# Low parts of streamed weights: a VectorE subtraction replaced by a negated copy on ScalarE and an accumulating DMA

## The chip, the cores and the metric

The kernel runs on one core of a Trainium2 chip. The metric is device time in microseconds of one execution. Three runs of the kernel before gave 1240.68, 1240.82 and 1240.99 us; the median is 1240.82 us.

A core has five engines with a queue each, which run their instructions in order and wait for one another by semaphores: TensorE (PE; its weight loads are shown as PEld), VectorE (DVE), ScalarE (ACT), GpSimd (POOL) and SyncE (SP), which here only issues DMAs. A DMA can be issued on SP, ACT or POOL; sixteen DMA engines move the data.

## The reference

The reference is a two-layer encoder trunk on one sequence of 512 tokens with 1024 features, in float32.

```python
for l in range(DEPTH):                       # DEPTH = 2
    h = rms_norm(x, norm1_g[l])
    proj = h @ w_in[l]                       # 1024 x 3584
    rq, rk, rv, rg, sq, sk, sv = jnp.split(proj, IN_SPLITS, axis=-1)
    ret = chunk_retention(apply_rotary(rq), apply_rotary(rk), rv)      # 4 heads of 128
    ret = head_group_norm(ret, ret_norm_g[l]) * jax.nn.silu(rg)
    sb = head_rms_norm(stick_breaking(sq, sk, sv), sb_norm_g[l])       # 4 heads of 128
    x = x + jnp.concatenate([ret, sb], axis=-1) @ w_out[l]             # 1024 x 1024
    h = rms_norm(x, norm2_g[l])
    x = x + (jax.nn.silu(h @ w_gate[l]) * (h @ w_up[l])) @ w_down[l]   # d_ff = 2816
return rms_norm(x, final_g)
```

## The kernel before

x is held transposed: eight tiles x[k] of 128 features by 512 tokens. Matrix products keep float32 precision by splitting each operand a into a high part (a rounded to the type fp32r, 12 bits of mantissa) and a low part (a minus the high part). A product is three matmuls: high by high, high by low, low by high (`mm3`). So TensorE needs the high part of a weight first and its low part with the second or third matmul of the first block.

All weights come in one stream, the tensor ws of 204 units; a unit is 128 partitions by 1024 columns of float32 (512 KB), in the order of use (`block_plan`, `unit_plan`). It holds eight blocks of 128x128, or two blocks of 128x512 where a weight is the moving operand (the value projections `proj_v`, and w_down in layer 1). `WeightStream.load` issues a unit's load on SP into one of three buffers wraw; `WeightStream.split` has ScalarE copy it to whi (line 124) and VectorE subtract whi from wraw into wlo (line 125); whi and wlo have three buffers each. `WeightStream.block` hands out the blocks. When the first block of unit u is asked for, it calls the split of the units up to u + 2 and the load of the one after. A buffer of whi or wlo is free when TensorE has used the last block of the unit three before.

The order of TensorE's work is fixed by the program (`Stream`): a main stream of projections, with the attention of each head put in as side tasks after a set delay. The order on the other engines is chosen by a scheduler when the kernel is built.

In most of the kernel TensorE uses the units one after the other. At the end of a `proj_v` and of each column half of w_down in layer 1, the last four blocks are used token block by token block, so that the results of a token block are complete early; the units of these four blocks (two of them, or three where the blocks don't begin at a unit's edge) are all held until the last token block:

```python
for f in fs[: FH - tail]:                 # tail = 4, FH = 11
    w = wst.block("w_down", l, f, dh * 512, 512)
    for tb in range(TB): step(tb, f, w)
rest = [(f, wst.block("w_down", l, f, dh * 512, 512)) for f in fs[FH - tail :]]
for tb in range(TB):
    for f, w in rest: step(tb, f, w)
```

The attention's own operands are split too. Those of q, k and the squares for the head norms have their low parts made on GpSimd (qlo, klo, slo), those of the score weights and the mixed heads on VectorE (ptlo, mlo). `mixed` (retention) computes m on VectorE (line 561), `normed` the square and its parts shi and slo (lines 460, 273, 274), which TensorE sums over the head with a matrix of ones (`finish`).

Of the kernel before, what the change touches and what calls it, by code (L numbers as in the profile page):

```python
# [10 lines left out]
F32 = mybir.dt.float32  # L11
F32R = mybir.dt.float32r
BF16 = mybir.dt.bfloat16
AF = mybir.ActivationFunctionType
ALU = mybir.AluOpType
# [18 lines left out]
BIG = float(2.0**100)  # L34
RQ, RK, RV, RG, SQ, SK, SV = (512 * i for i in range(7))

# the triangle of score blocks, by bank: block rows of [query, key], and of [key, query]
BY_QUERY = ((3,), (2, 0), (1,))
BY_KEY = ((0,), (1, 3), (2,))
WARM = 10  # L40
# [2 lines left out]


def block_plan():
    """Weight blocks in the order of their use: (tensor, layer, k tile, column, width)."""
    plan = []

    def cols(name, l, col):
        return [(name, l, k, col, P) for k in range(KT)]  # L50

    for l in range(L):
        plan += [("w_in", l, k, SV, 512) for k in range(KT)]
        for h in range(NH):
            for c in (SQ, SK, RG):
                plan += cols("w_in", l, c + h * HD)
        plan += [("w_in", l, k, RV, 512) for k in range(KT)]
        for h in range(NH):
            plan += cols("w_in", l, RQ + h * HD) + cols("w_in", l, RK + h * HD)
        for d in range(KT):  # L60
            plan += [("w_out", l, NH + k, d * P, P) for k in range(NH)]
        for d0 in range(0, KT, 4):
            ds = range(d0, d0 + 4)
            plan += [("w_out", l, k, d * P, P) for d in ds for k in range(NH - 1)]
            plan += [("w_out", l, NH - 1, d * P, P) for d in ds]
        for k in range(KT):
            for f in range(2):
                plan += [("w_gate", l, k, f * P, P), ("w_up", l, k, f * P, P)]
        for half in range(2):
            fs = range(half * FH, half * FH + FH)  # L70
            for f in fs:
                if f >= 2:
                    plan += cols("w_gate", l, f * P) + cols("w_up", l, f * P)
            if l < L - 1:
                for d in range(KT):
                    plan += [("w_down", l, f, d * P, P) for f in fs]
            else:
                for dh in range(2):
                    plan += [("w_down", l, f, dh * 512, 512) for f in fs]
    return plan  # L80
# [11 lines left out]


class WeightStream:
    """Loads the weights ahead of their use and splits each into two 12-bit parts."""

    AHEAD = 3

# [16 lines left out]
    def split(self, upto, step=UW):  # L115
        nc = self.nc
        self.load(upto)
        for i in range(len(self.ready), min(upto, len(self.units))):
            raw, w = self.raw[i]
            hi = self.pool.tile([P, UW], F32R, tag="whi", name=f"whi{i}", bufs=3)  # L120
            lo = self.pool.tile([P, UW], F32R, tag="wlo", name=f"wlo{i}", bufs=3)
            for a in range(0, w, step):
                c = slice(a, min(a + step, w))
                nc.scalar.copy(out=hi[:, c], in_=raw[:, c])  # L124
                nc.vector.tensor_tensor(  # L125
                    out=lo[:, c], in0=raw[:, c], in1=hi[:, c].bitcast(F32), op=ALU.subtract
                )
            self.ready.append((hi, lo))

    def block(self, *key):  # L130
# [9 lines left out]


class Stream:
    """The order of the tensor engine's work: side tasks are put into the main stream
    when enough of it has passed for their operands to be ready."""

    def __init__(self, nc):
        self.nc = nc
# [51 lines left out]
def layers(ctx, tc, xT_in, ws_in, gcol_in, gfin_in, cos_in, sin_in, dec_in, out):  # L199
    nc = tc.nc  # L200
# [8 lines left out]
    NG = 24  # L209

    def table(inst):
        """Keeps the scalar engine's table functions in the order of the program."""
        tc.stamp_issue_order_token(inst.ins, "table")
        return inst

# [15 lines left out]
    x = [keep.tile([P, S], F32, name=f"x{k}", tag=f"x{k}") for k in range(KT)]  # L231
    nc.sync.dma_start(out=x[0], in_=xT_in[:, 0, :])
    wst.load(1, step=512)
    for k in range(1, KT):
# [12 lines left out]
    eps = const.tile([P, 1], F32, name="eps")  # L247
# [4 lines left out]
        out=mask16, in_=mask16, compare_op=ALU.is_gt, fill=-BIG,  # L252
# [6 lines left out]
    rs = keep.tile([P, S], F32, name="rs")  # L259
# [20 lines left out]
            )  # L280

    def feed(k, g):
        """x tile k is complete: its gained and split copy, and its squares."""
        split(hhi[k], hlo[k], x[k], gcol[:, g + k : g + k + 1])
        if k == 0:
            nc.scalar.activation(out=ssq, in_=x[k], func=AF.Square)
        else:
            q = small.tile([P, S], F32, tag="sqx", name="sqx", bufs=2)
            nc.scalar.activation(out=q, in_=x[k], func=AF.Square)  # L289
            nc.gpsimd.tensor_tensor(out=ssq, in0=ssq, in1=q, op=ALU.add)  # L290

    def rsqrt(out, ss, n, act=nc.scalar.activation):
        """out = (ss / n + eps) ** -0.5, from exp and ln and a Newton step."""
        shape = list(ss.shape)
        tag = "" if shape[1] == S else str(shape[1])
        r = small.tile(shape, F32, tag="r" + tag, name="r" + tag, bufs=1)
        u = small.tile(shape, F32, tag="u" + tag, name="u" + tag, bufs=1)
        act(out=r, in_=ss, func=AF.Ln, scale=1.0 / n, bias=eps)
        act(out=r, in_=r, func=AF.Exp, scale=-0.5)
        nc.vector.scalar_tensor_tensor(  # L300
            out=u, in0=r, scalar=-0.5 / n, in1=r, op0=ALU.mult, op1=ALU.mult
        )
        nc.vector.scalar_tensor_tensor(
            out=u, in0=ss, scalar=n * EPS, in1=u, op0=ALU.add, op1=ALU.mult
        )
        nc.vector.scalar_tensor_tensor(
            out=out, in0=u, scalar=1.5, in1=r, op0=ALU.add, op1=ALU.mult
        )

    def token_scale():  # L310
        """rs[:, t] = rsqrt(mean of x[t]^2 + eps), the same on every partition."""
        hi, lo = (small.tile([P, S], F32R, tag="sqx", name=n, bufs=2) for n in ("sshi", "sslo"))
        split(hi, lo, ssq)
        ps = bank("o", 1)
        pe.mm(ps, ones_r, hi, True, False)
        pe.mm(ps, ones_r, lo, False, True)
        rsqrt(rs, ps, DM, act)
# [11 lines left out]
    def attention(l):  # L329
        g0 = l * NG  # L330
        with tc.tile_pool(name=f"at{l}", bufs=1, reuse_waits="tile") as sb:
# [23 lines left out]
                return ps  # L355

            def proj_v(col, evac):
                """[token, column] products, the last k tiles by token block."""
                pss = banks_a() if col == SV else [bank() for _ in range(3)] + [bank("z", 4)]
                v = [  # L360
                    sb.tile([P, TB, S], F32R, tag=n, name=n, bufs=1) for n in ("vhi", "vlo")
                ]

                def step(tb, k, w):
                    c = slice(tb * P, tb * P + P)
                    pe.mm3(pss[tb], (hhi[k][:, c], hlo[k][:, c]), w, k == 0, k == KT - 1)

                for k in range(KT - 4):
                    w = wst.block("w_in", l, k, col, 512)
                    for tb in range(TB):  # L370
                        step(tb, k, w)
                ws = [(k, wst.block("w_in", l, k, col, 512)) for k in range(KT - 4, KT)]
                done = []
                for tb in range(TB):
                    for k, w in ws:
                        step(tb, k, w)
                    done.append(tb)
                    if col == SV and tb == 0:
                        continue
                    if col == SV and tb == 1:  # L380
                        scales()
                    while done:
                        i = done.pop(0)
                        evac(i, pss[i], v[0][:, i], v[1][:, i])
                return v
# [33 lines left out]
                return parts(r, tag)  # L419

            def outer(ps, a, b, ca, cb, last=True):
                """ps = a[:, ca].T @ b[:, cb] for split a and b."""
                n = cb.stop - cb.start
                if n == P:
                    pe.mm(ps, a[0][:, ca], b[0][:, cb], True, last)
                else:
                    pe.mm(ps, a[1][:, ca], b[1][:, cb], True, False)
                    pe.mm(ps, a[1][:, ca], b[2][:, cb], False, False)
                    pe.mm(ps, a[2][:, ca], b[1][:, cb], False, last)
# [8 lines left out]
                return hi, lo  # L438

            def weighted(wt, v, h):  # L440
                """o[e, t] = sum over s of v[s, e] wt[s, t], by blocks of s."""
                o = bank("o", 1)
                e = slice(h * HD, h * HD + HD)
                for js, (hi, lo) in zip(BY_KEY, wt):
                    a = 0
                    for j in js:
                        c = slice(a, a + S - j * P)
                        a = c.stop
# [6 lines left out]
            mix = {}  # L455

            def normed(o, m, key):
                """m, o by head with its gains, times the rsqrt of o's mean squares."""
                sq = temp("sq")
                nc.scalar.activation(out=sq, in_=o, func=AF.Square)  # L460
                shi = sb.tile([P, S], F32R, tag="shi", name="shi", bufs=1)
# [335 lines left out]
```

## Time and profile before

| | |
|---|---|
| median of three runs | 1240.82 us |
| span of the profiled execution, first to last instruction | 1238.8 us |
| what the median has above that span | 2.0 us |
| TensorE busy | 1220.4 us, 99% |
| VectorE busy | 693.5 us, 56% |
| ScalarE busy | 488.8 us, 39% |
| GpSimd busy | 165.7 us, 13% |
| data moved by DMA | 115.74 MB, 93 GB/s |

Busy time says how much of the span an engine had an instruction in work. Matmuls overlap and their ends are modelled, so 99% does not mean that TensorE runs at its peak; it means that it hardly ever stands still. PEclk is the clock that TensorE was granted, as a share of full speed. The profiled execution is one of its own, with its span alone; the three timed runs are timed from outside and hold some 2 us around that span.

### The profile page before, as it was taken

How to read it: one execution, taken by the hardware profiler on the slowest of the kernel's cores; microseconds unless marked ns; L12 is line 12 of the kernel's file. 1: busy time of each engine (PE TensorE's matmuls, PEld its weight loads, DVE VectorE, ACT ScalarE, POOL GpSimd, SP SyncE). 2: the span in 40 equal slices, each digit the busy share in tenths (PEclk: the TensorE clock that was granted, in tenths of full speed). 3: DMA queues.
4: the chain of work that ended last, by engine and by line, in shares of the span. 5: the costliest groups of instructions: out<-in, count | busy, mean ns of one | idle time of the engine just before them, and what ended most of it. 6: DMA issues, size and time to landing. Idle time of an engine off the chain costs nothing.

```text
span 1238.8 us, 13898 instructions
## 1 busy us (share of the span) xinstructions
PE 1220.4 (99%) x5474; PEld 999.2 (81%) x5474; DVE 693.5 (56%) x861; ACT 488.8 (39%) x708; POOL 165.7 (13%) x142
## 2 busy tenths in 40 slices
PE   8999999999999999999999999999999999999997
PEld 5888887888888888888888888878888888888886
DVE  5557799775443244444444778997644433444433
ACT  5557553453322123223334766345432312223323
POOL 3221154130000000000112212422100000000011
PEclk9999999999999999999999999999999999999999
DMA  6221231232322323322232222223322322332221
GB/s 238 86 80 57 85 102 58 80 101 87 102 100 87 102 86 101 102 93 96 91 129 86 69 69 85 85 69 102 103 85 89 99 83 94 113 102 87 101 85 69
DMA packets 33329, 115.74 MB, mean 93 GB/s; under 512 B 3824, under 2 KB 3824, under 8 KB 33264
## 3 DMA queue, kind: packets, MB, share of 16 engines
q1 hardware_dynamic: 33120, 114.83, 28.1%
q8 instruction: 43, 0.70, 0.2%
q14 instruction: 22, 0.18, 0.0%
q10 hardware_dynamic: 144, 0.02, 0.0%
HBM read 112.75 MB, written 2.10 MB: 93 GB/s over the span
## 4 chain that ended last, share of the span: by engine, by line
PE 94%; DVE 4%; issue 1%; DMA 1%; ACT 1%; POOL 0%; SPq 0%; DVEq 0%; ACTq 0%
PE acc L178 72%; PE z L178 16%; PE o L178 5%; PE z L189 1%; DMA wraw<-ws 1%; DVE ptlo L274 1%; DVE wlo L125 1%; DVE hlo L277 0%; DVE u L300 0%; DVE mlo L274 0%; POOL slo L274 0%; DVE m L561 0%; DVE t L416 0%; DVE t L414 0%; DVE p L552 0%
## 5 line engine op out<-in xcount | busy, mean ns | idle before, releaser
L124 ACT CAST whi<-wraw 128x1024 fp32r<-128x1024 f32 (+1 forms) x205 | 214.6, 1047 | 505.7 <-PE acc L178 237.2
L178 PE MATMUL acc<-hhi,whi 128*128 128x512 f32 x960 | 376.0, 392 | 0.0
L178 PE MATMUL acc<-hhi,wlo 128*128 128x512 f32 x960 | 373.9, 389 | 0.0
L178 PE MATMUL acc<-hlo,whi 128*128 128x512 f32 x960 | 373.6, 389 | 0.0
L125 DVE TENSOR_TENSOR wlo<-wraw,whi 128x1024 fp32r<-128x1024 f32 (+1 forms) x205 | 258.1, 1259 | 135.8 <-ACT whi L124 134.7
L178 PEld LDWEIGHTS acc<-hhi,wlo 128*128 128x128 f32 x960 | 180.2, 188 | 37.8
L178 PEld LDWEIGHTS acc<-hhi,whi 128*128 128x128 f32 x960 | 180.3, 188 | 36.2
L178 PEld LDWEIGHTS acc<-hlo,whi 128*128 128x128 f32 x960 | 180.3, 188 | 36.0
L665 DVE TENSOR_TENSOR u<-acc,rs 128x512 f32<-128x512 f32 x40 | 27.7, 692 | 134.5 <-PE acc L178 134.5
L290 POOL TENSOR_TENSOR ssq<-ssq,sqx 128x512 f32<-128x512 f32 x28 | 44.8, 1600 | 397.0 <-ACT sqx L289 396.3
L662 DVE TENSOR_TENSOR g<-acc,rs 128x512 f32<-128x512 f32 x40 | 27.7, 692 | 89.9 <-PE acc L178 89.9
L178 PE MATMUL acc<-ahi,wlo 128*128 128x512 f32 x176 | 69.8, 396 | 0.0
L178 PE MATMUL acc<-alo,whi 128*128 128x512 f32 x176 | 69.8, 396 | 0.0
L178 PE MATMUL acc<-ahi,whi 128*128 128x512 f32 x176 | 69.8, 396 | 0.0
L730 POOL TENSOR_TENSOR xtd<-xtd,gfin 128x512 f32<-128x512 f32 x7 | 10.1, 1447 | 349.3 <-ACT fsq L726 349.3
L277 DVE SCALAR_TENSOR_TENSOR hlo<-x,gcol,hhi 128x512 fp32r<-128x512 f32 x32 | 38.6, 1224 | 9.0 <-ACT hhi L276 9.0
L178 PEld LDWEIGHTS acc<-alo,whi 128*128 128x128 f32 x176 | 33.1, 188 | 8.1
L178 PEld LDWEIGHTS acc<-ahi,whi 128*128 128x128 f32 x176 | 33.1, 188 | 8.1
L178 PEld LDWEIGHTS acc<-ahi,wlo 128*128 128x128 f32 x176 | 33.1, 188 | 8.1
L273 ACT CAST ahi<-u 128x512 fp32r<-128x512 f32 x44 | 27.3, 621 | 28.1 <-DVE u L666 28.1
L178 PE MATMUL acc<-mhi,wlo 128*128 128x512 f32 x88 | 36.2, 411 | 0.0
L178 PE MATMUL acc<-mlo,whi 128*128 128x512 f32 x88 | 36.0, 409 | 0.0
(189 smaller groups left out, 1819.0 us busy)
## 6 DMA issues: line engine op xcount, KB each, us to landing
wraw<-ws SPq DMA_DIRECT2D x203, 512.0 KB, 3.5
x<-xT SPq DMA_DIRECT2D x8, 256.0 KB, 7.4
dec<-dec SPq DMA_DIRECT2D x8, 256.0 KB, 4.1
out<-ob SPq DMA_DIRECT2D x4, 512.0 KB, 2.6
wraw<-ws SPq DMA_DIRECT2D x2, 256.0 KB, 3.8
cosrs<-cos SPq DMA_DIRECT2D x2, 256.0 KB, 5.3
sinrs<-sin SPq DMA_DIRECT2D x2, 256.0 KB, 5.4
gfin<-gfin SPq DMA_DIRECT2D x1, 512.0 KB, 4.5
```

Of the source, the lines that this page charges most:

```text
L124: nc.scalar.copy(out=hi[:, c], in_=raw[:, c])
L125: nc.vector.tensor_tensor(out=lo[:, c], in0=raw[:, c], in1=hi[:, c].bitcast(F32), op=ALU.subtract)
L178: self.nc.tensor.matmul(ps, lhsT=lhsT, rhs=rhs, start=start, stop=stop)
L189: self.nc.tensor.transpose(out, src, ident)
L273: nc.scalar.copy(out=hi, in_=src)
L274: eng.tensor_tensor(out=lo, in0=src, in1=hi.bitcast(F32), op=ALU.subtract)
L277: eng.scalar_tensor_tensor(out=lo, in0=src, scalar=scale, in1=hi.bitcast(F32), op0=ALU.mult, op1=ALU.subtract,)
L290: nc.gpsimd.tensor_tensor(out=ssq, in0=ssq, in1=q, op=ALU.add)
L662: nc.vector.tensor_tensor(out=g, in0=pg, in1=rs, op=ALU.mult)
L665: nc.vector.tensor_tensor(out=u, in0=pu, in1=rs, op=ALU.mult)
L730: nc.gpsimd.tensor_tensor(out=y, in0=y, in1=gfin[:, c], op=ALU.mult)
```

## The change

From unit 4 on the low part is made in another way. ScalarE writes the negated high part into wlo (a copy of wraw with the factor -1, which is rounded as the high part is). Then a DMA issued on GpSimd reads the unit from memory a second time and adds it to what stands in wlo. Units 0 to 3 keep the subtraction on VectorE. The loads into wraw stay; a wraw buffer is now free when ScalarE has read it twice.

```diff
                 nc.scalar.copy(out=hi[:, c], in_=raw[:, c])
-                nc.vector.tensor_tensor(
-                    out=lo[:, c], in0=raw[:, c], in1=hi[:, c].bitcast(F32), op=ALU.subtract
-                )
+                if i < 4:
+                    nc.vector.tensor_tensor(
+                        out=lo[:, c], in0=raw[:, c], in1=hi[:, c].bitcast(F32), op=ALU.subtract
+                    )
+                else:
+                    nc.scalar.activation(out=lo[:, c], in_=raw[:, c], func=AF.Copy, scale=-1.0)
+                    nc.gpsimd.dma_start(out=lo[:, c], in_=self.ws[i, :, c], accum_op=ALU.add)
             self.ready.append((hi, lo))
```

The rest of the diff only removes comments. Lines after 127 stand four lines further down in the changed kernel, so that line 273 is 277 there.

The scheduler places the new instructions among the others. ScalarE before, at the change of column halves in the last w_down (whi is a unit's high part, fsq the squares for the last norm, xtd the output by token block):

```order
L124 CAST whi_8844<-wraw_8818 128x1024 [waits DMAHW5_49,DVE_49,PE_49]
L726 ACTIVATE fsq,fss_6752<-xtd_6748 128x512 [waits DVE_49]
L726 ACTIVATE fsq,fss_6753<-xtd_6749 128x512 [waits DVE_49]
L124 CAST whi_8862<-wraw_8848 128x1024 [waits DMAHW6_49,PE_49,Activation_49]
L726 ACTIVATE fsq,fss_6754<-xtd_6750 128x512 [waits DVE_49,Activation_49]
L124 CAST whi_8868<-wraw_8866 128x1024 [waits DMAHW7_49,PE_49]
```

And now at the same place, where wlo on line 130 is the negated copy:

```order
L124 CAST whi_9038<-wraw_9012 128x1024 [waits PE_49,Activation_49]
L730 ACTIVATE fsq,fss_6888<-xtd_6884 128x512 [waits DVE_49]
L730 ACTIVATE fsq,fss_6889<-xtd_6885 128x512 [waits DVE_49]
L130 ACTIVATE wlo_9058<-wraw_9043 128x1024 [waits DMAHW6_49,DMASW0_49,PE_49]
L124 CAST whi_9057<-wraw_9043 128x1024 [waits PE_49,Activation_49]
L730 ACTIVATE fsq,fss_6890<-xtd_6886 128x512 [waits DVE_49,Activation_49]
L130 ACTIVATE wlo_9065<-wraw_9062 128x1024 [waits DMAHW7_49,DMASW1_49,PE_49]
```

Each unit has two instructions on ScalarE, and here the negated copy stands ahead of the high part; the order among the rest is the same.

GpSimd before, in the late attention of layer 0 (q and k are rotated queries and keys, qlo and klo their low parts, slo that of the squares of a head):

```order
L418 TENSOR_TENSOR k<-t_1701,t_1702 128x512 [waits DVE_49]
L274 TENSOR_TENSOR klo<-k,khi 128x512 [waits PE_49,Activation_49]
L418 TENSOR_TENSOR q<-t_1759,t_1760 128x512 [waits DVE_49,PE_49]
L274 TENSOR_TENSOR slo<-sq,shi 128x512 [waits Activation_49]
L274 TENSOR_TENSOR qlo<-q,qhi 128x512 [waits Activation_49]
```

And now at the same place:

```order
L131 DMA wlo_1738<-ws 128x1024 [waits DMASW5_49,Activation_49]
L422 TENSOR_TENSOR k<-t_1725,t_1726 128x512 [waits DVE_49]
L278 TENSOR_TENSOR klo<-k,khi 128x512 [waits Activation_49]
L131 DMA wlo_1797<-ws 128x1024 [waits DMASW6_49,Activation_49]
L422 TENSOR_TENSOR q<-t_1784,t_1785 128x512 [waits DVE_49,PE_49]
L278 TENSOR_TENSOR slo<-sq,shi 128x512 [waits Activation_49]
L278 TENSOR_TENSOR qlo<-q,qhi 128x512 [waits Activation_49]
```

The DMA issues stand among GpSimd's additions and subtractions, each with a wait for ScalarE's negated copy, and what comes after one in the queue starts after it.

## Rows read from the trace of the kernel before

**Rows 1.** The page's busy times of the engines, with share and number of instructions.

```profile
PE 1220.4 (99%) x5474; PEld 999.2 (81%) x5474; DVE 693.5 (56%) x861; ACT 488.8 (39%) x708; POOL 165.7 (13%) x142
```

**Rows 2.** Stretches of 4 us: length, busy times, granted clock, DMA share, GB/s.

```profile
192.00:196.00 4.00, 3.58 (x20) 2.97 (x19) 3.83 (x6) 1.55 (x2) 1.28 (x1) 1.00 0.24 97
200.00:204.00 4.00, 1.66 (x7) 0.85 (x6) 3.87 (x7) 3.68 (x7) 1.93 (x2) 1.00 0.16 67
204.00:208.00 4.00, 4.00 (x12) 3.13 (x11) 3.95 (x5) 1.50 (x3) 1.24 (x1) 0.57 0.02 8
...
808.00:812.00 4.00, 1.66 (x6) 0.88 (x5) 3.87 (x7) 4.00 (x8) 2.30 (x2) 0.98 0.05 20
812.00:816.00 4.00, 4.00 (x12) 3.08 (x12) 3.57 (x4) 1.13 (x2) 0.86 (x1) 0.59 0.17 30
```

**Rows 3.** Timeline, 188 to 204: start, length, engine, line, tiles, [idle before <-releaser].

```profile
188.96 1.23 DVE L125 TENSOR_TENSOR wlo<-wraw,whi 128x1024 fp32r<-128x1024 f32 x1
...
196.65 1.23 DVE L125 TENSOR_TENSOR wlo<-wraw,whi 128x1024 fp32r<-128x1024 f32 x1
...
199.49 0.74 DVE L561 SCALAR_TENSOR_TENSOR m<-o,gcol,gate 128x512 f32<-128x512 f32 x1
...
202.07 1.47 POOL L274 TENSOR_TENSOR slo<-sq,shi 128x512 fp32r<-128x512 f32 x1 [3.06 <-ACT shi L273]
...
203.60 0.50 PE L178 MATMUL o<-slo,ones_r 128*128 128x512 f32 x1 [1.05 <-POOL slo L274]
```

**Rows 4.** Groups by shape: xcount, busy us, mean ns, idle us before and releasers.

```profile
L125 DVE TENSOR_TENSOR wlo<-wraw,whi 128x1024 fp32r<-128x1024 f32 x203 | 256.8, 1265 | 135.5 <-ACT whi L124 134.5
...
L124 ACT CAST whi<-wraw 128x1024 fp32r<-128x1024 f32 x203 | 213.5, 1052 | 505.7 <-PE acc L178 237.2 <-issue 176.6 <-PE z L178 58.4
```

**Rows 5.** DMA: queue with packets, MB, share; issues; the tile wraw's landing times.

```profile
q1 hardware_dynamic: 33120, 114.83, 28.1%
...
wraw<-ws SPq DMA_DIRECT2D x203, 512.0 KB, 3.5
...
DMA to landing us min/median/max: 3.3/3.5/8.3
```

**Rows 6.** SP's waits (us in total, times, longest), and its issues: ns min/median/max.

```profile
SPq L112 <- DVE wlo L125: 1088.4, 197, 12.3
...
L112 SPq DMA_DIRECT2D wraw<-ws x205: 327/328/749, 1.2 to 1203.1; - x103
```

**Rows 7.** Timeline of ScalarE in the feed-forward part of layer 0.

```profile
322.62 1.05 ACT L124 CAST whi<-wraw 128x1024 fp32r<-128x1024 f32 x1 [3.86 <-issue]
...
328.06 1.05 ACT L124 CAST whi<-wraw 128x1024 fp32r<-128x1024 f32 x1 [3.11 <-PE acc L178]
```

**Rows 8.** Timeline at the change of column halves, w_down of layer 1.

```profile
1017.18 1.05 ACT L124 CAST whi<-wraw 128x1024 fp32r<-128x1024 f32 x1 [10.85 <-DVE xtd L723]
...
1022.12 0.40 PE L178 MATMUL z<-wlo,ahi 128*128 128x512 f32 x1
```

**Rows 9.** Timeline after two proj_v of layer 0, and after w_down's first half.

```profile
35.19 1.05 ACT L124 CAST whi<-wraw 128x1024 fp32r<-128x1024 f32 x1
...
41.90 0.39 PE L178 MATMUL acc<-hhi,wlo 128*128 128x512 f32 x1
...
145.48 1.05 ACT L124 CAST whi<-wraw 128x1024 fp32r<-128x1024 f32 x1
...
152.51 0.39 PE L178 MATMUL acc<-hhi,wlo 128*128 128x512 f32 x1
...
1048.68 1.05 ACT L124 CAST whi<-wraw 128x1024 fp32r<-128x1024 f32 x1 [8.75 <-PE z L178]
...
1055.78 0.39 PE L178 MATMUL acc<-hhi,wlo 128*128 128x512 f32 x1
```

**Rows 10.** Timeline of the fourth stick-breaking head of layer 0: GpSimd, then TensorE.

```profile
112.97 1.65 POOL L274 TENSOR_TENSOR klo<-k,khi 128x512 fp32r<-128x512 f32 x1 [5.59 <-ACT khi L273]
...
116.05 0.40 PE L178 MATMUL z<-klo,qhi 128*128 128x512 f32 x1
```

## The prediction, made before the changed kernel ran

> **What bounds the kernel now.** I read the page's busy table first: TensorE is busy 99% of the span, VectorE 56%, ScalarE 39%, GpSimd 13% [rows 1]. So the time is TensorE's matmul stream plus the few places where it stops or runs at its lower clock, and an edit to another engine counts only where TensorE waits for it. The table of stretches shows the largest such place: at the end of each attention part TensorE is idle for some 2.3 us, and in the 4 us after that its granted clock is 0.57 to 0.59, a fall towards the lower of its two levels [rows 2]. The timeline says who is late there: VectorE, whose queue holds a weight subtraction (wlo, line 125) at 188.96 and another at 196.65, then the product m at 199.49; from m come the square and its split slo on GpSimd, and TensorE starts only when slo ends [rows 3]. Everywhere else the weights are early: in the feed-forward part ScalarE copies a unit's high part every 5.44 us, for use two units later [rows 7].
>
> **What goes.** From unit 4 on, 200 of the 204 units lose a subtraction of 1.265 us [rows 4], 253 us of VectorE. Nearly all of it lies beside TensorE's work and is worth nothing. In the late stretch two of them, 2 x 1.23 us, stand before m [rows 3]. Without them m, slo and TensorE come up to 2.46 us earlier, against 0.42 + 2.34 = 2.76 us of idle time in layer 0, and 2.34 in the last stretch of layer 1 [rows 2]. If the stop shrinks to a few tenths the clock should not fall either: 4 us x (1 - 0.57) = 1.7 us more. That bounds the gain at about 4.2 us a layer, 8.3 in all; the lower bound is nothing, if slo comes late for another reason. I take 3.5 a layer, 7 in all, because a few tenths of the wait are not covered. The subtraction that TensorE waits for at the start belongs to unit 3, which keeps it.
>
> **What is added.** ScalarE gets 200 negated copies of 128x1024. Its cast of that shape takes 1.052 us [rows 4], so 210 us more, and ScalarE goes from 39% to 56% busy. GpSimd gets 200 DMA issues. The DMA engines get 200 x 512 KB from memory again, plus a read of the same 512 KB in the destination, since an addition into the destination needs both. The important part is latency. Before, a low part was ready about 1.2 us after its high part. Now it is ready when the negated copy is written, GpSimd has issued, and the DMA has landed. I call the last two together T.
>
> T has no row. A plain load of the same size lands in 3.5 us, between 3.3 and 8.3 [rows 5]. Its packets take 0.281 x 1238.8 x 16 / 33120 = 0.168 us; at 9 packets for each engine that is 1.5 us of moving data [rows 5]. The second read adds 1.5. SP's load of a later unit waits for line 125 today, 197 times [rows 6], so it will wait for the negated copy and start at the same moment as the accumulation; sharing the 16 engines adds another 1.5. An issue takes 0.33 us on SP [rows 6]; I put 0.3 for GpSimd's. T = 3.5 + 1.5 + 1.5 + 0.3 = 6.8 us. The bounds are the plain load's own 3.3 and its worst 8.3; above that an addition that moves slowly through the DMA engines cannot be excluded by any row. I take 6.8, as the sum of the parts. Data volume alone doesn't bind: 28.1% x 3 = 84% of the engines' time.
>
> The Trainium skill (DMA: Bandwidth & Descriptors, Anatomy of one DMA — SWDGE (gpsimd) path) fits a DMA issued on GpSimd as 2.0 us plus its bytes over 436 GB/s, an estimate of 3.2 us for 512 KB. No run here shows such a DMA; the plain loads on SP, at 3.5, agree with it within a tenth. With 3.2 for T nothing below would be late; that is the first rival's world.
>
> **Where T is covered and where not.** In the steady stream a unit's buffer comes free two units before its successor is wanted: 2 x 5.44 us less high and negated copy (2.1) leaves 8.8 us for T [rows 7]. So 6.8 is hidden in most of the kernel. It is not where a block of matmuls holds two or three of the three buffers to its end, which happens in seven places, each time with the negated copy placed first on ScalarE:
> - w_down of layer 1, between the two column halves (two places). ScalarE starts the next unit at 1017.18 and TensorE wants its low part at 1022.12 [rows 8]; less 1.05 for the copy and 0.1 for a semaphore, 3.8 us are left. Short by 3.0 us each, 6.0. A stop of that size brings the clock down as in [rows 2], 1.7 each, 3.4.
> - After proj_v of the stick-breaking heads, both layers: 35.19 to 41.90 [rows 9], 5.55 left, short by 1.25, 2.5 in both.
> - After proj_v of the retention heads, both layers: 145.48 to 152.51 [rows 9], 5.9 left, short by 0.9, 1.8 in both.
> - From w_down's first half to the gate columns in layer 1: 1048.68 to 1055.78 [rows 9], 5.95 left, short by 0.85.
> Together 6.0 + 3.4 + 2.5 + 1.8 + 0.85 = 14.6 us.
>
> The DMA issue also stands in GpSimd's queue and waits there for ScalarE's negated copy; behind it are the splits qlo, klo and slo, for which TensorE waits. In the tightest of four heads klo ends at 114.62 and is wanted at 116.05 [rows 10]: 1.4 us of cover, against 1.05 for a negated copy ahead of khi and 0.3 for the issue. That I cost at nothing; if an issue holds GpSimd for 1 us, it costs 0.6 us in each layer. In the late attention stretch the negated copy stands on ScalarE before mhi, in time that is idle there, so it does not delay slo.
>
> The sum, made on the profiled span: 1238.8 - 7 + 14.6 = 1246.4. The median of the runs is 2.0 above that span, so about 1248.5 by the median; 1248 is predicted, some 0.6% slower.
>
> **Rivals.**
> First, the accumulation lands like a plain load: T of 3.3 to 4.3. For it: the fixed part of 3.5 us is by far the larger one, and rows show no cost of an addition. Against it: two streams have to be read and the raw load starts beside it. Then the seven places cost under 1 us and the relief of VectorE stays: 1240.8 - 7 = 1234, or 1232.5 with the full 8.3.
>
> Second, T of about 5, no contention with the raw load. Two places are short by 1.2, with one clock fall each at most: 2.4 + 3.4 - 7 = -1.2, so 1239.6, no difference to be told (0.2%, 2.5 us, is about what a measurement of this kernel tells from no change).
>
> Third, on the slow side, the accumulating DMA is slow enough to bound the stream: T above 8.8. Each buffer then turns once in 16.3 + (T - 8.8) us, so every unit costs (T - 8.8) / 3 more, over some 180 units. At T = 9: 12 us, and the seven places 38, less 7: 1284. At T = 10: 72 + 46 - 7, so 1352. The DMA engines themselves bind when an added DMA takes more than (100 - 28.1) / 28.1 = 2.6 times the packet time of a plain one; I assumed twice, which is near. Against it: each of the 16 engines has only some 32 KB to add for each unit.
>
> **How the numbers follow.** Forecast, T between 6 and 8: 0.40, from 1243 (T = 6: 9 - 7) to 1265 (T = 8: 31 - 7). First rival 0.24, second 0.15, third 0.21. Faster by over 0.2%: the first rival and a little of the second, 0.27. Within 0.2%: the rest of the second and the foot of the forecast, 0.14. Slower: the forecast and the third rival, 0.59. The range has to reach the first rival at 1232 and into the third, up to T just over 9: 1300. The forecast's own range is 1243 to 1265.
>
> **What would show it.** In the profile after: the DMA table has a second 512 KB row issued on GpSimd, whose time to landing plus issue is T; 6 to 8 is right, under 5 or over 9 wrong. TensorE waits with an accumulating DMA as the releaser, longest in the two column-half changes of w_down in layer 1, near 1018 and 1200, by some 3 us, and a clock row near 0.6 behind each. The idle time near 200 and 810 us is down to a few tenths, with the clock staying at 1.0. ScalarE near 56%, VectorE near 36%. Waits of TensorE for klo or slo would show that GpSimd's queue, not T, is what costs. Waits for the low part in every feed-forward unit would be the third rival; none at all in the seven places the first.

## The result and the profile after

The changed kernel takes 1276.2 us (median of four runs, 1274.1 to 1278.1), against 1240.75 us for the kernel before on the same chip: 1.0289 times as long, 95% interval 1.0273 to 1.0306, or 35.5 us slower. Predicted were 1248 us. The direction is the predicted one; the loss is nearly five times the predicted 7.2 us, and the time lies above the forecast's own range, 1243 to 1265. The four runs of the changed kernel form two pairs, near 1274.2 and 1278.1 us, and the profiled execution, with a span of 1276.3 us, belongs to the longer pair.

The busy times, which answer to [rows 1], came out near what was expected for ScalarE and VectorE (53% and 35% for 56% and 36%):

```profile
PE 1231.4 (96%) x5474; PEld 1002.8 (79%) x5474; DVE 442.7 (35%) x661; ACT 670.2 (53%) x908; POOL 321.8 (25%) x342
```

The DMA table, which answers to [rows 5] (queue with packets, MB and share; issues with count, size and median us to landing), and the view of the tile wlo with its landing times, in us from the start of GpSimd's issue:

```profile
q0 software_dynamic: 28800, 104.87, 46.7%
...
wraw<-ws SPq DMA_DIRECT2D x203, 512.0 KB, 6.3
wlo<-ws POOLq DMA_DIRECT2D x200, 512.0 KB, 7.7
```

```profile
DMA to landing us min/median/max: 5.2/7.7/10.2
```

A packet of the accumulation holds a DMA engine for 0.467 x 1276.3 x 16 / 28800 = 0.331 us, twice the 0.168 us of a plain one, as the prediction assumed. The landing takes 7.7 us at the median. The plain load that runs beside it went from 3.5 to 6.3 us. The issue itself is a row on GpSimd (columns as in [rows 4]):

```profile
L131 POOL DMA_DIRECT2D wlo<-ws x200 | 173.8, 869 | 780.2 <-ACT wlo L130 766.0
```

What TensorE waited for (us in total, times, longest), first the view of the whole span and then of the last 276 us alone:

```profile
PE acc L182 <- DMA wlo<-ws: 13.0, 8, 4.2
PE z L182 <- DMA wlo<-ws: 10.1, 5, 3.3
PE o L182 <- POOL slo L278: 3.6, 4, 1.5
...
PE z L182 <- ACT khi L277: 2.8, 2, 1.4
PE z L182 <- POOL klo L278: 1.4, 2, 0.7
```

```profile
PE acc L182 <- DMA wlo<-ws: 8.5, 4, 4.2
PE z L182 <- DMA wlo<-ws: 7.7, 3, 3.3
```

So 16.2 of the 23.1 us of waiting for accumulations lie after 1000 us, nearly all of it in w_down of layer 1. The timeline there (start, length, engine, line, tiles, [idle before <-releaser]) names the places:

```profile
1025.05 0.50 PE L182 MATMUL acc<-wlo,ahi 128*128 128x512 f32 x1 [1.59 <-DMA wlo<-ws]
...
1028.76 0.50 PE L182 MATMUL acc<-wlo,ahi 128*128 128x512 f32 x1 [2.06 <-DMA wlo<-ws]
...
1043.74 0.50 PE L182 MATMUL z<-wlo,ahi 128*128 128x512 f32 x1 [2.81 <-DMA wlo<-ws]
...
1065.38 0.50 PE L182 MATMUL z<-wlo,ahi 128*128 128x512 f32 x1 [1.64 <-DMA wlo<-ws]
...
1222.18 0.50 PE L182 MATMUL acc<-wlo,ahi 128*128 128x512 f32 x1 [4.20 <-DMA wlo<-ws]
...
1239.15 0.50 PE L182 MATMUL z<-wlo,ahi 128*128 128x512 f32 x1 [3.27 <-DMA wlo<-ws]
```

Those at 1043.74 and 1239.15 are the changes of column halves that the prediction named ([rows 8]). The other four are inside a column half, where the four held blocks begin. None of them was predicted.

Stretches (columns as in [rows 2]): the late attention, the feed-forward part, and the 4 us behind the first change of column halves.

```profile
200.00:204.00 4.00, 4.00 (x22) 3.48 (x21) 3.87 (x8) 2.82 (x6) 2.19 (x3) 1.00 0.70 173
204.00:208.00 4.00, 4.00 (x19) 3.25 (x18) 2.92 (x2) 2.85 (x4) 2.91 (x3) 1.00 0.45 86
320.00:360.00 40.00, 40.00 (x179) 33.10 (x178) 9.00 (x13) 17.67 (x21) 6.05 (x7) 1.00 0.88 196
...
1044.00:1048.00 4.00, 4.00 (x13) 3.15 (x13) 0.00 (x0) 0.00 (x0) 0.00 (x0) 0.65 1.04 271
```

The stop near 200 us is gone and the clock stays up there. In the feed-forward part TensorE is busy for 40.00 of 40 us: the steady stream is covered. Behind the long stop at 1043.74 the clock is granted at 0.65.

The order of TensorE's matmuls is the same in both kernels, so the start times of the same matmul in the two traces can be set side by side. The difference grows or shrinks in steps. The steps, in us, with the clock's part inside:

| place | predicted | measured |
|---|---|---|
| the seven places of the prediction: column-half changes 9.7, ends of proj_v SV 4.0 and RV 1.7, gate 0.9 | +14.6 | +16.3 |
| starts of the held blocks in w_down of layer 1 | 0 | +11.8 |
| start of layer 1, in proj_v of the stick-breaking heads, near 630 to 645 | 0 | +4.9 |
| slo of stick-breaking heads | 0 | +4.7 |
| stop in the late attention goes, both layers | -7 | -9.8 |
| khi and klo of the next head, 10 us later, both layers | 0 | +8.5 |
| sum | +7.6 | +36.4 |

The spans differ by 1276.3 - 1238.8 = 37.5; 1.1 us is in steps too small to place. With those steps counted to the place where they lie, single rows move by up to half a microsecond (12.3 for 11.8, -10.3 for -9.8). The steps are those of one execution, too: of the last row, some 3 us are falls of the clock behind khi, and experiments 7 and 8, with the same waits of 1.4 us there, show none; the stop of 4.20 us at 1222.18 is 2.8 and 2.0 us at the same matmul in these two, whose w_down is unchanged.

### The profile page after: what moved, and what is told of

Read it like the earlier page. It is cut to its first block, busy times and chain, and to the rows that moved or that the text cites. A ratio compares the mean times of both kernels' runs of the same rounds, so it can differ in the third digit from the quotient of the medians.

```text
span 1276.3 us, 14285 instructions
## 1 busy us (share of the span) xinstructions
PE 1231.4 (96%) x5474; PEld 1002.8 (79%) x5474; DVE 442.7 (35%) x661; ACT 670.2 (53%) x908; POOL 321.8 (25%) x342
## 3 DMA queue, kind: packets, MB, share of 16 engines
q0 software_dynamic: 28800, 104.87, 46.7%
## 4 chain that ended last, share of the span: by engine, by line
PE 60%; issue 24%; DMA 5%; POOL 5%; ACT 3%; DVE 3%; SPq 0%; POOLq 0%; ACTq 0%; DVEq 0%
PE acc L182 47%; PE z L182 9%; DMA wlo<-ws 5%; POOL wlo L131 4%; PE o L182 3%; ACT wlo L130 1%; PE z L193 1%; DMA wraw<-ws 1%; ACT whi L124 0%; DVE hlo L281 0%; DVE m L475 0%; DVE e L508 0%; POOL slo L278 0%; DVE u L304 0%; DVE x L610 0%
## 5 line engine op out<-in xcount | busy, mean ns | idle before, releaser
L131 POOL DMA_DIRECT2D wlo<-ws x200 | 173.8, 869 | 780.2 <-ACT wlo L130 766.0
L130 ACT ACTIVATE wlo<-wraw 128x1024 fp32r<-128x1024 f32 x200 | 210.9, 1055 | 79.0 <-PE z L182 43.9
L294 POOL TENSOR_TENSOR ssq<-ssq,sqx 128x512 f32<-128x512 f32 x28 | 40.3, 1440 | 33.1 <-ACT sqx L293 31.8
L709 DVE TENSOR_TENSOR x<-x,acc 128x512 f32<-128x512 f32 x16 | 11.0, 687 | 95.2 <-PE acc L182 95.2
L182 PE MATMUL z<-wlo,ahi 128*128 128x512 f32 x88 | 36.5, 415 | 7.7 <-DMA wlo<-ws 7.7
L278 DVE TENSOR_TENSOR alo<-u,ahi 128x512 fp32r<-128x512 f32 x44 | 30.4, 692 | 35.5 <-ACT ahi L277 35.3
L182 PE MATMUL z<-wlo,hhi 128*128 128x512 f32 x80 | 33.4, 418 | 5.8 <-DVE wlo L126 3.3
```

Of the source, the lines that this page charges most:

```text
L130: nc.scalar.activation(out=lo[:, c], in_=raw[:, c], func=AF.Copy, scale=-1.0)
L131: nc.gpsimd.dma_start(out=lo[:, c], in_=self.ws[i, :, c], accum_op=ALU.add)
L182: self.nc.tensor.matmul(ps, lhsT=lhsT, rhs=rhs, start=start, stop=stop)
L278: eng.tensor_tensor(out=lo, in0=src, in1=hi.bitcast(F32), op=ALU.subtract)
L709: nc.vector.tensor_tensor(out=x[d], in0=x[d], in1=ps, op=ALU.add)
```

## The experiments

Every run is compared with the kernel before on the same chip. Below, "the changed kernel" is the one of the diff, and a run's span is set against its span of 1276.3.

**1. Two blocks held and not four.** In three of the four column halves of w_down; the last keeps four.

```diff
-                    tail = 4
+                    tail = 4 if half == 1 and dh == 1 else 2
```

> The changed kernel, but in w_down of layer 1 (all but the last column half) only the last two blocks are used token block by token block, not the last four, so that one or two weight buffers are held, not three. Theory H (the stops come where held buffers leave less than issue plus landing of an accumulating DMA, about 8 us, and this includes the start of the held stretch, which the prediction left out): the stops in w_down go, some 20 of the 21.6 us that the two traces differ by there, so about 1255 us, and no wait of TensorE for an accumulating DMA between 1000 and 1045. Rival B (the DMA engines, 76% busy, are late by themselves, wherever the buffers stand): the stops move but stay, less than 8 us gained, above 1268.

Measured: 1252.58 us, 1.0102 [1.0085, 1.0119]; the span is 25.9 us shorter. The waits for accumulations after 1000 us are down from 16.2 us to a single one (waits of TensorE, the same view as above):

```profile
PE acc L182 <- DMA wlo<-ws: 0.3, 1, 0.3
```

The landing is still 7.7 us. Of the 25.9 us, 3.4 lie outside w_down, in the first 36 us and in the clock behind khi, where the edit changes nothing. So it is not the stream that is too slow; what costs is that four blocks are wanted together while they hold the buffers.

**2. The same edit without the accumulation.** The kernel before, with the same line changed.

> Control: the kernel before, with VectorE's subtraction, but two blocks and not four held to the end in three of the four column halves of w_down in layer 1. Theory: holding costs nothing where the low part is ready 1.2 us after the high part, so within 0.2% of 1240.8 us, and the 23.6 us that the same edit gave the changed kernel are the accumulation's. Rival G (fewer held blocks help any kernel): 1225 to 1236.

Measured: 1240.03 us, 0.9998 [0.9988, 1.0007]. Holding four blocks costs nothing while a low part is ready 1.2 us after its high part, so the 24 us of experiment 1 belong to the accumulation.

**3. VectorE's subtraction back in w_down of layer 1 alone.**

```diff
-                if i < 4:
+                if i < 4 or any(b[0] == "w_down" and b[1] == L - 1 for b in self.units[i]):
```

> The changed kernel, but the units that hold w_down of layer 1 keep the subtraction on VectorE. By the two traces 21.6 us were lost there and 0.9 in the unit after it. Theory H: about 1253 us, the rest of the ledger unchanged. Rival B (the DMA engines' load as a whole): the other stops shrink or grow as well, and the time differs from 1253 by over 4 us.

Measured: 1255.18 us, 1.0119 [1.0104, 1.0134]; the span is 22.9 us shorter. Two edits that share nothing but the place give the same 23 to 26 us. The table's steps for w_down come to 9.7 + 11.8 = 21.5, and what lies above that is within the scatter of the runs.

**4. No accumulating DMA.** ScalarE's second pass stays, the DMA is taken out, so that the raw weights are never added.

```diff
-                    nc.gpsimd.dma_start(out=lo[:, c], in_=self.ws[i, :, c], accum_op=ALU.add)
```

> The changed kernel without the accumulating DMAs: ScalarE writes the negated high part and TensorE uses that as the low part, so the raw weights are not added (left out of the computation). What remains is ScalarE's second pass and the relief of VectorE. Theory H: all stops for accumulating DMAs go with the clock behind them, some 33 us, and the gain of the late attention stays in part: 1238 to 1243 us. Rival A (ScalarE's 211 us of extra work is a cause by itself): above 1250.

Measured: 1237.99 us, 0.9985 [0.9975, 0.9994]. The raw loads land in 3.5 us again. What is left of the losses comes with ScalarE's second pass and with the order that the scheduler now gives to the attention's own work (experiment 7 and the section after the experiments):

```profile
PE o L181 <- POOL slo L277: 2.3, 4, 0.9
PE z L181 <- POOL klo L277: 1.4, 2, 0.7
...
PE z L181 <- ACT khi L276: 1.0, 2, 0.5
```

**5. The same DMAs, but copying.** The destination is overwritten.

```diff
-                    nc.gpsimd.dma_start(out=lo[:, c], in_=self.ws[i, :, c], accum_op=ALU.add)
+                    nc.gpsimd.dma_start(out=lo[:, c], in_=self.ws[i, :, c], accum_op=ALU.bypass)
```

> The DMAs on GpSimd stay, at the same places and of the same size, but overwrite their destination and don't add to it (this leaves out the subtraction: the low parts become the raw weights). Theory A (the addition costs the DMA engines a second pass): the time of a packet falls from 0.331 us to that of a plain load, 0.168, the landing from 7.7 to about 5.5 us, the raw load's beside it from 6.3 to about 4.5, and with T some 2 us shorter the stops of TensorE for these DMAs shrink by about 2 us each: the clock falls less and the time is 1248 to 1256 us, with the stops for slo, klo and khi left. Rival C (the path by GpSimd is slow in itself, whatever is done with the data): landing stays at 7 us or more and the time above 1268.

Measured: 1243.0 us, 1.0018 [1.0009, 1.0027], below the range that was expected. The view of the tile wlo (issues in ns, landings in us, both min/median/max), then the DMA table:

```profile
L131 POOL DMA_DIRECT2D wlo<-ws x200: 527/528/720, 24.1 to 1216.8; - x100
...
DMA to landing us min/median/max: 3.7/4.5/6.9
```

```profile
q0 software_dynamic: 28800, 104.87, 24.1%
...
wraw<-ws SPq DMA_DIRECT2D x203, 512.0 KB, 3.5
wlo<-ws POOLq DMA_DIRECT2D x200, 512.0 KB, 4.5
```

With the same bytes from memory and the same queue, a packet takes 0.241 x 1241.1 x 16 / 28800 = 0.166 us, the landing 4.5 us, the raw load its old 3.5, and TensorE has no wait for these DMAs. So adding, where this run overwrites, makes 0.331 of 0.166 us a packet, 7.7 of 4.5 us to landing, and 1.0289 of 1.0018 in time, some 33 us. The second read with its issues costs some 4 us (1.0018 against 0.9985 in experiment 4).

The Trainium skill (DMA: Bandwidth & Descriptors, Anatomy of one DMA — SWDGE (gpsimd) path) gives 3.2 us for such a DMA as an estimate from its fit; here it is 4.5 us for the copy, counted from the start of an issue of 0.53, and 7.7 us for the addition. The measurement decides.

**6. Units accumulated by halves.** Two negated copies and two DMAs of 256 KB.

```diff
-                    nc.scalar.activation(out=lo[:, c], in_=raw[:, c], func=AF.Copy, scale=-1.0)
-                    nc.gpsimd.dma_start(out=lo[:, c], in_=self.ws[i, :, c], accum_op=ALU.add)
+                    for h in (slice(0, 512), slice(512, UW)):
+                        nc.scalar.activation(out=lo[:, h], in_=raw[:, h], func=AF.Copy, scale=-1.0)
+                        nc.gpsimd.dma_start(out=lo[:, h], in_=self.ws[i, :, h], accum_op=ALU.add)
```

> The changed kernel with each negated copy and each accumulating DMA in two halves of 256 KB. Theory (the landing is 3 us of fixed time and the rest data that has to pass the DMA engines twice): the first half lands in about 5.5 to 6 us, 2 us before the whole did, and its blocks are used first; the second lands about with the whole of before; the stops at the starts of held blocks and at the column halves shrink by 1 to 2 us each: 1255 to 1268 us. Rival I (the landing is fixed time or sharing with the raw load, not size): both halves land in over 7 us, and GpSimd issues 400 instead of 200 at 0.87 us, so slo and klo come later still: 1276 to 1290.

Measured: 1256.23 us, 1.014 [1.0123, 1.0157]. The time is in the theory's range, but neither account of the landing holds: 3.7 to 10.1 us, 7.4 at the median of all; the first halves land in 6.9 us at the median and not in 5.5 to 6, the second in 7.7. The stops inside w_down shrank; GpSimd's issues and ScalarE's copies now delay the attention more (timeline, TensorE):

```profile
1021.19 0.50 PE L183 MATMUL acc<-wlo,ahi 128*128 128x512 f32 x1 [0.24 <-DMA wlo<-ws]
...
216.20 0.80 PE L183 MATMUL z<-qhi,khi 128*128 128x512 f32 x1 [3.31 <-ACT khi L278]
```

How much of 7.7 us is fixed and how much is data isn't settled by this run, since two landings overlap.

**7. The attention's own splits on VectorE.** qlo, klo and slo leave GpSimd's queue.

```diff
-                split(hi, lo, t, eng=nc.gpsimd)
+                split(hi, lo, t)
...
-                split(shi, slo, sq, eng=nc.gpsimd)
+                split(shi, slo, sq)
```

> The changed kernel, but the low parts qlo, klo and slo are subtracted on VectorE, so that GpSimd's queue holds them no longer behind DMA issues. Theory Q (the two stops for slo and klo, and the loss right after the gain in the late attention, come from GpSimd's queue: issue of 0.87 us and work behind it): slo's 2 x 1.8 and 2 x 0.5 us and klo's 2 x 1.0 with some 3 us of clock go, about 1267 us. Rival A (they come from ScalarE, where the negated copy stands ahead of shi and khi): less than 2 us gained, 1274 or more.

Measured: 1268.08 us, 1.0229 [1.0213, 1.0244]; the span is 11.1 us shorter. All four waits for slo are gone, which by the steps is 4.6 us. Another 3.0 are falls of the clock behind khi that don't come here, and 4.1 lie in w_down, where there is nothing for the edit to move; small steps go the other way. So the waits bear out the theory for slo, and not the time, which agrees with it by luck. The wait for khi stays and klo's moves to VectorE:

```profile
PE z L182 <- ACT khi L277: 2.8, 2, 1.4
PE z L182 <- DVE klo L278: 1.5, 2, 0.8
```

So slo is late by the way through GpSimd, and khi is something else. In the changed kernel, at the first stick-breaking head, the queues are these (timelines of ScalarE, GpSimd and TensorE):

```profile
86.44 1.06 ACT L130 ACTIVATE wlo<-wraw 128x1024 fp32r<-128x1024 f32 x1
87.39 0.61 ACT L277 CAST qhi<-q 128x512 fp32r<-128x512 f32 x1
87.90 0.62 ACT L277 CAST shi<-sq 128x512 fp32r<-128x512 f32 x1
```

```profile
87.79 0.86 POOL L131 DMA_DIRECT2D wlo<-ws  x1 [5.28 <-ACT wlo L130]
88.36 1.62 POOL L278 TENSOR_TENSOR qlo<-q,qhi 128x512 fp32r<-128x512 f32 x1
89.61 1.58 POOL L278 TENSOR_TENSOR slo<-sq,shi 128x512 fp32r<-128x512 f32 x1
```

```profile
91.25 0.49 PE L182 MATMUL o<-slo,ones_r 128*128 128x512 f32 x1 [1.53 <-POOL slo L278]
```

A negated copy stands before qhi and shi, a DMA issue before qlo and slo, and TensorE waits 1.53 us. The order has changed too: unlike at the places shown with the change, the scheduler has here turned it round. In the kernel before, slo stood ahead of qlo on GpSimd, and shi ahead of qhi on ScalarE:

```profile
83.97 1.80 POOL L274 TENSOR_TENSOR slo<-sq,shi 128x512 fp32r<-128x512 f32 x1 [4.68 <-ACT shi L273]
85.73 1.29 POOL L274 TENSOR_TENSOR qlo<-q,qhi 128x512 fp32r<-128x512 f32 x1
```

Experiment 4, which has the copy and the new order but no issue, shows a wait of 0.94 us at this place, so the issue is the smaller part of it. Experiment 6 has the order of before, two copies and two issues, and waits 0.75. No run changes the order alone.

**8. The tables of layer 1 loaded later.** At 622 to 624 us SP issues four loads of 256 KB (tables of the rotation and of the decay). The edit makes each wait for a result of this layer.

```diff
                     if col == SV and tb == 0:
+                        if l == L - 1:
+                            for t in (cosrs, sinrs):
+                                nc.vector.tensor_copy(out=t[:, 0:1], in_=pss[0][:, 0:1])
                         continue
...
+                if l == L - 1 and h < 2:
+                    nc.vector.tensor_copy(out=dec[:, 0:1], in_=gate[:, h, 0:1])
                 nc.sync.dma_start(out=dec, in_=dec_in[:, h, :])
```

> The changed kernel, but in layer 1 the tables of the rotation and of the decay (4 x 256 KB) are loaded after the first token block of the stick-breaking value projection and later, not beside it. Theory: TensorE's stops at 627 to 641 us come from these loads, which share the DMA engines with the accumulations (landing 9.0 to 9.9 us there, 7.7 elsewhere); then the landings there fall to about 7.7 and the stops, 4.9 us with the clock, go nearly whole: about 1271 to 1273 us. Rival F (they come from the three units held by the end of the projection, or from GpSimd's sums of squares in front of the DMA issues): the stops stay, 1275 to 1278.

Measured: 1274.1 us, 1.0274 [1.026, 1.0288], against 1.0289 [1.0273, 1.0306]: unclear by the times. By the trace, the three accumulations issued at 622.00, 627.66 and 632.13 landed after 9.7, 9.9 and 9.0 us in the changed kernel, and after 8.1, 7.5 and 7.3 here. TensorE's step near 631 is gone and the clock doesn't fall at 641, but there 1.6 of 2.0 us remain, and the end of the projection, 20 us later, now costs 4.2 us where it cost 2.0. So the tables explain the longer landings. What they cost in time is not shown: the two places together cost 7.0 us in the changed kernel and 5.9 here, but 6.9, 6.7 and 6.1 in experiments 1, 3 and 7, where the tables are loaded as ever; in 1 and 3 the clock's fall, too, comes at the end of the projection and not at 641. Some 1 us at most is the tables'; that the rest comes from the start of the held blocks, as in w_down, is argued and no run tests it.

**9. Accumulation for four units alone.** The first two units of w_out in each layer, whose subtractions stood at 188.96 and 196.65 [rows 3]; all others keep VectorE.

```diff
-                if i < 4:
+                if i < 4 or any(b[0] != "w_out" or b[2] < NH or b[3] >= 512 for b in self.units[i]):
```

> The accumulating DMA only for the four units whose subtraction stood before the late heads in VectorE's queue (the first two of w_out for the stick-breaking heads in each layer); all other units keep the subtraction on VectorE. Theory: the gain of 4.9 us a layer at the end of attention is due to these two subtractions alone and stays whole, since no negated copy stands before khi and no DMA issue before klo and slo any more; so 1240 - 9.8 = about 1230 us, faster than both. Rival D (the gain comes from VectorE being free for the whole attention part): a gain under 2 us a layer, 1236 to 1240. Rival E (the copies and issues of these units alone already delay khi and klo of the last retention head): the 4.9 is given back by half, about 1235.

Measured: 1231.99 us, 0.993 [0.9918, 0.9943]. It beats both kernels. The late stretch in layer 0, and the norm's matmul that stood at 203.60 [rows 3]:

```profile
200.00:204.00 4.00, 4.00 (x19) 3.26 (x18) 4.00 (x4) 2.27 (x3) 2.28 (x2) 1.00 0.33 65
204.00:208.00 4.00, 4.00 (x19) 3.23 (x18) 3.94 (x7) 0.88 (x1) 0.00 (x0) 1.00 0.34 131
```

```profile
201.34 0.39 PE L182 MATMUL o<-slo,ones_r 128*128 128x512 f32 x1
```

No wait stands behind it, and TensorE has none for khi or klo. The stop goes as in the changed kernel, 5.1 us a layer by the steps; 0.4 us a layer comes back soon after and 1.2 us is lost in the first 30 us, which leaves 8.1 of the span and 8.5 by the medians. So the gain comes from two subtractions a layer. The four accumulations run almost alone here, each with one or two plain loads beside it, and land no sooner (view of the tile wlo):

```profile
DMA to landing us min/median/max: 6.6/8.1/8.3
```

So the landing of 7.7 us in the changed kernel is not due to the load of its 200 accumulations on the DMA engines. The plain loads beside these four landed in 3.8 to 4.2 us.

**10. The same four units on GpSimd.** The kernel before; no accumulating DMA at all.

```diff
-                nc.vector.tensor_tensor(
+                late = all(b[0] == "w_out" and b[2] >= NH and b[3] < 512 for b in self.units[i])
+                (nc.gpsimd if late else nc.vector).tensor_tensor(
```

> The kernel before, with the subtraction of the same four units as in the run with four accumulations (the first two of w_out for the stick-breaking heads in each layer) on GpSimd and not on VectorE; no accumulating DMA at all. Theory: the gain of some 9 us comes from taking these four off VectorE and is had without the DMA if GpSimd has the room; a subtraction of 128x512 takes it 1.47 us, so one of 128x1024 about 2.9, and it idles 3.06 us before slo: 1231 to 1234 us. Rival H (the subtraction stands in GpSimd's queue before k, klo or slo and delays the same score and norm matmuls): half or all of the gain is lost, 1236 to 1242.

Measured: 1233.03 us, 0.9944 [0.9929, 0.9959], not to be told from experiment 9. TensorE's wait for slo is gone, one of 0.8 us for klo is left in each layer. The subtraction takes GpSimd 2.4 to 2.6 us:

```profile
186.88 2.59 POOL L126 TENSOR_TENSOR wlo<-wraw,whi 128x1024 fp32r<-128x1024 f32 x1
```

## Why the prediction was wrong in size

**What goes: right, and low.** The stop went, with the clock's fall, and gave 9.8 us for the 7 predicted. Experiment 9 has it without the rest.

**T: right as a mechanism, 1.2 us short.** Landing 7.7 and 0.3 from the copy's end to the issue make 8.0 us; predicted were 6.8, with the packet time as assumed. The plain load beside it shares in the cost, as the sum's term for sharing said: three accumulations with a plain load beside them for 1.1 us or not at all landed in 5.2 to 6.4 us, where the sum without that term has 5.3. The first rival's world did not come; nor did the third rival's, since the steady stream is covered up to 8.8.

**The seven places: right, and the size partly by luck.** 16.3 us for 14.6. The longest are the column-half changes, 2.8 and 3.3 us of wait with a clock of 0.65 behind the first. But by the prediction's own figures a T of 8 costs 31 us there. At these places T was only 7.0 to 7.5 us, and the cover, from the copy's end to the moment when TensorE stood ready, was 4.3, 5.8, 6.6 and 6.4 us where 3.8, 5.55, 5.9 and 5.95 had been worked out. The two errors nearly cancel.

**The step that failed is "Where T is covered and where not", in its sentence that 6.8 is hidden in most of the kernel except at the seven places.** It took 8.8 us of cover for every unit up to the end of a held stretch. But where the four held blocks begin, TensorE takes all four for one token block, 12 matmuls or 2.8 us, before it comes to the next, where a stream of units takes 5.44 us each. The second and third unit are wanted early, while their predecessors keep the buffers. At the four stops of this kind in w_down the cover, counted in the same way, was 8.5, 6.1, 6.4 and 4.5 us, for a T of 10.0, 8.1, 8.0 and 8.7; at 1222.18, for example, the copy had ended at 1213.46 and TensorE stood ready at 1217.98. That cost 11.8 us in w_down and, as far as can be argued, most of the 4.9 us in layer 1. Experiments 1 and 3 take the loss in w_down away, together with that of the two column-half changes, which shares its cause, and experiment 2 shows that the edit of experiment 1 gives the kernel before nothing. They don't part the start of a held stretch from its end; only the steps of the two traces do.

**"That I cost at nothing" failed too.** The prediction measured GpSimd's cover at klo of the fourth stick-breaking head [rows 10]. The tight place was slo of the first, and the prediction's own bound for an issue that holds GpSimd for 1 us, 0.6 us a layer, was below the 2.4 us a layer that came, most of it with the negated copy and the new order and not with the issue. Experiment 7 takes slo's share away.

**The gain was given back.** The prediction stopped at slo and did not ask what is late next. Ten microseconds on, TensorE came to khi 4.9 us earlier and found it late. Why khi was late stands in the timelines. First VectorE in the kernel before, then VectorE, GpSimd, ScalarE and TensorE in the changed one:

```profile
211.80 0.69 DVE L471 TENSOR_TENSOR m<-m,rn 128x512 f32<-128x512 f32 x1
212.41 0.68 DVE L606 TENSOR_TENSOR x<-x,acc 128x512 f32<-128x512 f32 x1
```

```profile
213.77 0.69 DVE L610 TENSOR_TENSOR x<-x,acc 128x512 f32<-128x512 f32 x1
214.37 2.17 DVE L475 TENSOR_TENSOR m<-m,rn 128x512 f32<-128x512 f32 x1
```

```profile
213.79 0.86 POOL L131 DMA_DIRECT2D wlo<-ws  x1 [5.17 <-ACT wlo L130]
214.35 1.63 POOL L422 TENSOR_TENSOR k<-t,t 128x512 f32<-128x512 f32 x1
```

```profile
216.57 0.62 ACT L277 CAST mhi<-m 128x512 fp32r<-128x512 f32 x1 [3.09 <-DVE m L475]
217.10 0.61 ACT L277 CAST khi<-k 128x512 fp32r<-128x512 f32 x1
```

```profile
217.76 0.50 PE L182 MATMUL z<-qhi,khi 128*128 128x512 f32 x1 [1.38 <-ACT khi L277]
```

Two things have changed. The scheduler has put VectorE's addition x ahead of the product m, where m stood first, so m can begin only when x ends, at 214.46, and GpSimd is then at work on its DMA issue and on k. And the issue delays k. The product ends 0.56 us after k does, 2.17 us after its recorded start, where it took 0.69 before. ScalarE has mhi, which needs m, ahead of khi in its queue, so khi is late and klo follows it.

The runs part the two. In all eight with x ahead of m (the changed kernel and experiments 1 and 3 to 8) m ends 0.55 to 0.56 us after k; in the four with m ahead (the kernel before and experiments 2, 9 and 10) it takes 0.69 us and TensorE has no wait for khi. Experiment 4, experiment 5 and the changed kernel have the same order and differ in the issue before k, which takes nothing, 0.53 and 0.87 us: TensorE waits 0.49, 1.03 and 1.38 us for khi, so the issue is passed on in full and 0.5 us remain without it. No run moves x alone.

## What to carry over

A longer latency in a stream of buffers is priced at each place where the order of use changes, at its start as well as at its end: ask how soon after the first held unit the last is wanted, and when its buffer came free. Before work is moved off an engine everywhere, find the few instructions that the bottleneck waits for; here four of 200 carried the whole gain, and the other 196 only brought cost. A change of instructions lets the scheduler order the other queues anew: compare the order on every engine at each place where the bottleneck waits, and not at one or two. When a stop is taken away, follow the next matmuls on the path until one of them waits for something that the change also touched.

## What the runs showed of the hardware that was not expected

An accumulating DMA of 512 KB takes twice the DMA engines' time of a copy (0.331 and 0.166 us a packet) and holds GpSimd longer for its issue (0.87 and 0.53 us). As a stream it nearly doubles the landing of the plain loads (6.3 us where the copies left them at 3.5); the four lone ones of experiment 9 brought the loads beside them to 3.8 to 4.2 us.

VectorE and GpSimd held each other up for most of an instruction: where m was first (the kernel before), m took 0.69 us and k 1.80; where k was first (experiment 4, k at 210.01, m at 210.56), k took 1.29 and m 1.28, with its end 0.55 us behind k's. The Trainium skill (SBUF — State Buffer, Who interferes with whom) says that issue order decides which of the two engines waits for the shared port. These rows agree, but the recorded start does not tell who was first: in experiment 7 m is recorded 0.04 us ahead of k and still takes 2.24 us. Its start lies before the end of x, the instruction ahead of it, and counted from there, 0.04 us after k's start, it comes second.
